# A two-layer diffusion trunk: conditioning transposes leave the fixed order of TensorE, their bias loads move up, the last norm is spread over three engines

## The chip, the core and the metric

The kernel runs on one core of a Trainium2 chip. The core has five engines with queues of their own: TensorE (PE, matrix products and transposes), VectorE (DVE), ScalarE (ACT), GpSimd (POOL) and SyncE (SP), whose queue issues most of the DMA transfers here. The metric is the device time of one execution in microseconds (us); less is better.

## The reference

The reference is a trunk of two layers over 512 latent tokens and 256 context tokens of width 1024. Each layer modulates a layer norm by a conditioning vector (adaLN), projects, runs four groups of heads side by side, projects back, adds a residual with a second norm, and then runs a modulated squared-ReLU MLP with a residual and a norm. Cut to what the change touches:

```python
def modulate(x, shift, scale):
    return layer_norm(x) * (1 + scale) + shift

mod = silu(c) @ w_ada + b_ada          # six vectors of 1024 per layer and stream
h = modulate(x, shift_1, scale_1)
y = concat(pool(h), windowed attention(h), latent attention(h), spatial gating(h)) @ w_out
x = layer_norm(alpha * x + gate_1 * y) * ln1_g + ln1_b
h = modulate(x, shift_2, scale_2)
x = layer_norm(alpha * x + gate_2 * (relu(h @ w_1) ** 2 @ w_2)) * ln2_g + ln2_b
```

The output is the latent stream behind layer two.

## The kernel before

All is float32. A product is made of three passes over parts `hi` and `lo` of both operands (`mm3`; every product has the line L133, every transpose L188, since helpers record them). Tokens are tiled by 128.

**Mixers.** The two attention groups run as units: one unit is one block of 128 queries of two heads, 24 units in layer 0 (latents and context) and 16 in layer 1 (latents alone). Loop pass x makes the scores of unit x (`s` and `sm`), transposes the probabilities of unit x-1 (`pT`), and makes the values of unit x-2 (`o`). `todo` holds projections of the latent attention (`uq`, `uk`) and the rotary work, each due at some x. `firsts[3]` is the unit at which the last pair of heads begins: 18 in layer 0, 12 in layer 1.

**Filler.** In each pass `fill(x, n)` also takes steps of `conditioning()`: a step loads 512 KB of the conditioning weights (`wada`, through SP's queue into one of four `raw` buffers) and makes 8 products `ada` of it. There are 40 steps in layer 0 and 24 in layer 1, paced so that they are spent two units ahead of the end. Sixteen steps make a block, for part of ada2 eight. At a block's end DVE adds the bias (`adaA = ada + badab`, L259; `badab` is loaded by four small DMAs, into a slot of the pool "T"), and `ada_cols` transposes the result into columns: up to four transposes `adaT` into one bank of PSUM, each copied out by DVE (`mc`, L275). Layer 0 has three blocks in its mixers, layer 1 two.

**What sets the order.** A scheduler orders each engine's instructions by its own estimates, except where the kernel chains them. While `self.pin` is set, every product and transpose is chained to the one before it in the order of the code (`pinned`), and the mixers set it for the whole loop. The pool `pa` has three PSUM banks of the tag "A", and `adaT`, `pT`, `uq`, `uk`, `o` and `wo` all draw on it. SP's queue runs in order: a load that waits for a free `raw` buffer holds up all that stand behind it, such as `rawwo` (weights of the output projection) and `rawz` (weights of the MLP).

**The last norm.** Behind the last MLP product each of four latent tiles takes: `fft = ff * gate` (DVE, L1266), `x += fft` (POOL for the last tiles, else DVE, L1267), statistics (L180, L182), the power -1/2 on POOL, then `affine_ln`: two operations on DVE per half (L328: subtract the mean, times g; L332: times the reciprocal deviation, plus b), and two DMAs of the output on SP's queue. `modT` transposes and modulates a normed tile, and ACT writes the result twice: rounded (`hi`, L377) and in full (`hfull`, L380).

The lines in which the block's bias and the pace stand:

```python
if u == 3 and i == len(part) - 1:
    bt = self.T("badab").rearrange("p (q x) -> p q x", q=4)
    for j in range(4):
        self.load(...)
wt = self.pr.tile([128, 2, 512], F32, name=self.nm("wada"), tag="raw")
...
want = (x + 1) * (24 if last else 40) // (n - 2) + 1
```

## Time and profile before

| | before |
|---|---|
| median of 3 runs | 1595.63 us (1595.61 to 1597.77) |
| profiled execution: time | 1597.13 us |
| profiled execution: span of the core | 1595.0 us |
| PE busy | 1496.2 us (94%) |
| DVE, ACT, POOL busy | 917.0, 567.1, 217.6 us |
| PE idle in the windows 160 to 320 us (mixers, layer 0) | 26.8 us |
| PE idle in the windows 1040 to 1200 us (mixers, layer 1) | 20.5 us |
| mean granted clock of PE | 0.974 |

The span runs from the first to the last instruction of the profile; the time of an execution has some 2 us more. Start times below count from the span's start. The granted clock is a share of the full 2.4 GHz: 1.00 is 2.4 and 0.50 is 1.2 GHz. An idle time in square brackets is the time for which the engine stood still just ahead of the instruction, with what released it.

### The profile page before, as it was taken

The numbers are of one execution on the slowest core, as the hardware profiler recorded it, in microseconds if no ns is written. First come the engines' busy times: TensorE is split into PE (matmuls) and PEld (weight loads), VectorE is DVE, ScalarE is ACT, GpSimd is POOL, SyncE is SP. The second block draws the span as 40 slices with busy tenths as digits, with TensorE's granted clock in tenths as the row PEclk, the third lists the DMA queues.
The fourth block names the chain that finished last, engine by engine and source line by source line (L and its number), as shares of the span: only waits on it lengthen the run. The fifth ranks groups of instructions, "written<-read, shape, count | busy, mean of one in ns | idle before, by whom it ended". The sixth has DMA issues, their size and how long they took to land. (4 is left out here: it accounts for less than half of the span.)

```text
span 1595.0 us, 23455 instructions
## 1 busy us (share of the span) xinstructions
PE 1496.2 (94%) x9438; PEld 1256.5 (79%) x9438; DVE 917.0 (57%) x1596; ACT 567.1 (36%) x1016; POOL 217.6 (14%) x243
## 2 busy tenths in 40 slices
PE   5999889799999999999999989979798999999996
PEld 3789667687898888888888868867676888888885
DVE  4484755547545455354554798666555555655557
ACT  4533444433731221212213157345434523223230
POOL 1011333213000000000000061143223000000003
PEclk9999899899999999999999999989899999999999
DMA  8531344652422122221212223224554333332321
GB/s 303 149 114 60 113 151 156 188 198 92 115 93 66 54 68 65 66 67 54 78 56 66 80 93 110 63 93 141 165 174 137 120 105 93 94 94 91 106 79 53
DMA packets 148068, 169.92 MB, mean 107 GB/s; under 512 B 8776, under 2 KB 96248, under 8 KB 147960
## 3 DMA queue, kind: packets, MB, share of 16 engines
q1 hardware_dynamic: 138488, 150.98, 30.5%
q10 hardware_dynamic: 9472, 17.45, 3.2%
q8 instruction: 74, 1.21, 0.3%
q14 instruction: 34, 0.28, 0.1%
HBM read 164.19 MB, written 4.22 MB: 106 GB/s over the span
## 5 line engine op out<-in xcount | busy, mean ns | idle before, releaser
L162 ACT ACTIVATE hiw<-raww 128x1024 fp32r<-128x1024 f32 x120 | 127.1, 1065 | 565.1 <-PE ff L133 565.1
L165 DVE TENSOR_TENSOR low<-raww,hiw 128x1024 fp32r<-128x1024 f32 x120 | 146.4, 1222 | 246.2 <-ACT hiw L162 246.2
L133 PE MATMUL ff<-low,fh 128*128 128x512 f32 x640 | 249.0, 389 | 0.0
L133 PE MATMUL ff<-hiw,fl 128*128 128x512 f32 x640 | 249.0, 389 | 0.0
L133 PE MATMUL ff<-hiw,fh 128*128 128x512 f32 x640 | 247.9, 389 | 0.0
L133 PE MATMUL ff<-hl,hiw 128*128 128x512 f32 (+1 forms) x672 | 237.9, 354 | 0.0
L133 PE MATMUL ff<-hh,hiw 128*128 128x512 f32 (+1 forms) x672 | 237.8, 354 | 0.0
L133 PE MATMUL ff<-hh,low 128*128 128x512 f32 (+1 forms) x672 | 237.7, 354 | 0.0
L1266 DVE TENSOR_TENSOR fft<-ff,gate 128x512 f32<-128x512 f32 x160 | 109.8, 686 | 100.3 <-PE ff L133 100.3
L133 PEld LDWEIGHTS ff<-hh,hiw 128*128 128x128 f32 x672 | 127.1, 189 | 18.0
L133 PEld LDWEIGHTS ff<-hl,hiw 128*128 128x128 f32 x672 | 127.1, 189 | 17.7
L133 PEld LDWEIGHTS ff<-hh,low 128*128 128x128 f32 x672 | 127.0, 189 | 17.5
L133 PEld LDWEIGHTS ff<-hiw,fl 128*128 128x128 f32 x640 | 120.2, 188 | 25.0
L133 PEld LDWEIGHTS ff<-hiw,fh 128*128 128x128 f32 x640 | 120.2, 188 | 24.8
L133 PEld LDWEIGHTS ff<-low,fh 128*128 128x128 f32 x640 | 120.2, 188 | 24.5
L1267 POOL TENSOR_TENSOR x<-x,fft 128x512 f32<-128x512 f32 x16 | 23.2, 1456 | 846.1 <-DVE fft L1266 841.1
L133 PE MATMUL ada<-wada,sc 128*32 128x128 f32 x1536 | 62.6, 302 | 26.1 <-DMA wada<-in_w_ada 26.1
L540 POOL TENSOR_SCALAR p<-p,rec 128x768 f32<-128x768 f32 (+3 forms) x80 | 60.9, 765 | 170.0 <-DVE rec L539 153.6
L1267 DVE TENSOR_TENSOR x<-x,fft 128x512 f32<-128x512 f32 x112 | 77.3, 690 | 2.9
L133 PEld LDWEIGHTS ada<-wada,sc 128*32 128x32 f32 x1536 | 42.5, 118 | 41.8 <-DMA wada<-in_w_ada 20.5
L133 PE MATMUL wo<-lowo,yh 128*128 128x512 f32 x160 | 62.5, 390 | 0.6 <-DVE lowo L165 0.6
L133 PE MATMUL wo<-hiwo,yh 128*128 128x512 f32 x160 | 62.4, 394 | 0.6 <-ACT hiwo L162 0.6
(331 smaller groups left out, 2761.4 us busy)
## 6 DMA issues: line engine op xcount, KB each, us to landing
raww<-in_w_ff SPq DMA_DIRECT2D x120, 512.0 KB, 4.2
wada<-in_w_ada SPq DMA_DIRECT2D x96, 512.0 KB, 4.2
rawwo<-in_w_out SPq DMA_DIRECT2D x16, 512.0 KB, 8.7
rawz<-in_w_ff SPq DMA_DIRECT2D x8, 512.0 KB, 6.7
rawwb<-in_w_in SPq DMA_DIRECT2D x12, 256.0 KB, 5.3
gate<-grow ACTq DMA_DIRECT2D x6, 512.0 KB, 4.7
badab<-in_b_ada SPq DMA_DIRECT2D x36, 64.0 KB, 4.6
x<-in_x SPq DMA_DIRECT2D x4, 512.0 KB, 4.2
```

The source lines that it names most:

```text
L133: return self.pinned(self.nc.tensor.matmul(out, lhsT, rhs, start=start, stop=stop))
L162: i = nc.scalar.activation(out=hi, in_=raw, func=AF.Copy)
L165: nc.vector.tensor_tensor(out=lo, in0=raw, in1=hi.bitcast(F32), op=ALU.subtract)
L540: nc.gpsimd.tensor_scalar(out=p[:, :keep], in0=p[:, :keep], scalar1=rec, scalar2=1.0, op0=ALU.mult, op1=ALU.mult)
L1266: nc.vector.tensor_tensor(out=t, in0=ps, in1=g[:, sl], op=ALU.mult)
L1267: eng.tensor_tensor(out=xt[:, sl], in0=xt[:, sl], in1=t, op=ALU.add)
```

## The change

1. `ada_cols` clears `self.pin` around its transposes and sets it again behind them: the chain runs past them, and the scheduler places them.
2. The four loads of a block's bias are issued at u = 0 of the block's last column piece, not at u = 3, so three steps earlier.
3. `load_heads` (weights of the latent attention's head projections) is called ahead of `sgu`, and splits a whole weight in two instructions on ACT and two on DVE, not in so many for each 128 of its rows.
4. The rotary work is due at x = 1 instead of 0, and what is due is now done behind `fill`.
5. `fill` is paced by `firsts[3]` (18 and 12) instead of n - 2 (22 and 14).
6. `modT` can share: for all calls but the first of the latents, every second full copy is made by DVE instead of ACT.
7. `affine_ln`: ACT scales and shifts, DVE multiplies by g, and b is added by POOL for the first half (by DVE for the second half, and for the last tile); the second half's output goes out through ACT's queue; the last tile's `x += fft` is on DVE.

```diff
                 for u in range(4):
-                    if u == 3 and i == len(part) - 1:
+                    if u == 0 and i == len(part) - 1:
                         bt = self.T("badab").rearrange("p (q x) -> p q x", q=4)
...
         nc = self.nc
+        pin, self.pin = self.pin, None
         if mc is None:
...
                 )
+        self.pin = pin
         return mc
...
-    def affine_ln(self, x, g, b):
+    def affine_ln(self, x, g, b, end):
         nc = self.nc
         m, rs = self.stats(lambda i: x[:, 512 * i:512 * i + 512], 2, EPS_R)
-        hs = [slice(512 * i, 512 * i + 512) for i in range(2)]
-        for h in hs:
-            nc.vector.scalar_tensor_tensor(
-                out=x[:, h], in0=x[:, h], scalar=m, in1=g[:, h], op0=ALU.subtract, op1=ALU.mult
-            )
-        for h in hs:
-            nc.vector.scalar_tensor_tensor(
-                out=x[:, h], in0=x[:, h], scalar=rs, in1=b[:, h], op0=ALU.mult, op1=ALU.add
-            )
+        nb = self.neg_mean(m, rs)
+        for i in range(2):
+            h = slice(512 * i, 512 * i + 512)
+            nc.scalar.activation(out=x[:, h], in_=x[:, h], func=AF.Identity, scale=rs, bias=nb)
+            nc.vector.tensor_tensor(out=x[:, h], in0=x[:, h], in1=g[:, h], op=ALU.mult)
+            eng = nc.vector if i or end else nc.gpsimd
+            eng.tensor_tensor(out=x[:, h], in0=x[:, h], in1=b[:, h], op=ALU.add)
...
-    def modT(self, xn, t0, t1, shift, scale, h, kts=range(KT), two=False):
+    def modT(self, xn, t0, t1, shift, scale, h, kts=range(KT), two=False, share=False):
...
             )
-            nc.scalar.activation(out=full[:, :n], in_=pt[:, :n], func=AF.Identity, scale=sc, bias=sh)
+            if share and kt % 2:
+                nc.vector.tensor_scalar(
+                    out=full[:, :n], in0=pt[:, :n], scalar1=sc, scalar2=sh, op0=ALU.mult, op1=ALU.add
+                )
+            else:
+                nc.scalar.activation(out=full[:, :n], in_=pt[:, :n], func=AF.Identity, scale=sc, bias=sh)
             nc.vector.tensor_tensor(out=lo, in0=full[:, :n], in1=hi.bitcast(F32), op=ALU.subtract)
...
+        def load_heads(src, cut, wide, name):
+            raw = self.pr.tile([128, src.shape[1], 4 * wide], F32, name=self.nm("raw" + name), tag="raw")
+            self.load(out=raw, in_=src)
+            hi, lo = (
+                self.pw.tile([128, src.shape[1], 4 * wide], F32R, name=self.nm(t + name), tag="W")
+                for t in ("hi", "lo")
+            )
+            r = raw.rearrange("p k (h c) -> p k h c", c=wide)
+            for a, b in ((0, cut), (cut, wide)):
+                h, w = (
+                    t[:, :, 4 * a:4 * b].rearrange("p k (h c) -> p k h c", c=b - a) for t in (hi, lo)
+                )
+                nc.scalar.activation(out=h, in_=r[:, :, :, a:b], func=AF.Copy)
+                nc.vector.tensor_tensor(
+                    out=w, in0=r[:, :, :, a:b], in1=h.bitcast(F32), op=ALU.subtract
+                )
+            return hi, lo
+        Wq = load_heads(A["mla_w_uq"][l].rearrange("(k p) n -> p k n", p=128), 64, 96, "uq")
+        Wk = load_heads(A["mla_w_ukv"][l].rearrange("(k p) n -> p k n", p=128), 64, 128, "ukv")
...
-        def load_heads(src, cut, wide, name):
-            raw = self.pr.tile([128, src.shape[1], 4 * wide], F32, name=self.nm("raw" + name), tag="raw")
-            self.load(out=raw, in_=src)
-            hi, lo = (
-                self.pw.tile([128, src.shape[1], 4 * wide], F32R, name=self.nm(t + name), tag="W")
-                for t in ("hi", "lo")
-            )
-            for k in range(src.shape[1]):
-                r = raw[:, k, :].rearrange("p (h c) -> p h c", c=wide)
-                for a, b in ((0, cut), (cut, wide)):
-                    h, w = (
-                        t[:, k, 4 * a:4 * b].rearrange("p (h c) -> p h c", c=b - a) for t in (hi, lo)
-                    )
-                    nc.scalar.activation(out=h, in_=r[:, :, a:b], func=AF.Copy)
-                    nc.vector.tensor_tensor(out=w, in0=r[:, :, a:b], in1=h.bitcast(F32), op=ALU.subtract)
-            return hi, lo
-        Wq = load_heads(A["mla_w_uq"][l].rearrange("(k p) n -> p k n", p=128), 64, 96, "uq")
-        Wk = load_heads(A["mla_w_ukv"][l].rearrange("(k p) n -> p k n", p=128), 64, 128, "ukv")
         VM = [self.X([128, 4, 256], "vmL"), self.X([128, 2, 256], "vmC")]
...
-        todo = {0: [rotary]}
+        todo = {1: [rotary]}
...
                 self.out_part(yL)
-            for st in todo.pop(x, []):
-                st()
             if x == n + 1:
...
                 values(x - 2)
-            fill(x, n)
+            fill(x, firsts[3])
+            for st in todo.pop(x, []):
+                st()
             if g is not None:
...
                     for n in range(2):
-                        ff2_tile(fs, Ws[n], n, tl, nc.gpsimd, self.last_mm if j + n else None)
+                        eng = nc.vector if l == DEPTH - 1 and j == len(tiles) - 1 else nc.gpsimd
+                        ff2_tile(fs, Ws[n], n, tl, eng, self.last_mm if j + n else None)
                     done(j)
...
             def fill(x, n):
-                want = (x + 1) * (24 if last else 40) // (n - 2) + 1
+                want = (x + 1) * (24 if last else 40) // n + 1
                 while spent[0] < want and next(steps, 0) is None:
...
                 self.modT(lambda i, kt: self.xn_cols(xn1[o + i], kt), t0, t1,
-                          col(mc[1], 8, s), col(mc[2], 0, s), hC if s else hL)
+                          col(mc[1], 8, s), col(mc[2], 0, s), hC if s else hL, share=s or t0 > 0)
...
                 if last:
-                    self.affine_ln(t, g2, b2)
-                    for h in (slice(0, 512), slice(512, 1024)):
-                        nc.sync.dma_start(out=self.out[128 * j:128 * j + 128, h], in_=t[:, h])
+                    self.affine_ln(t, g2, b2, j == LT - 1)
+                    for h, q in ((slice(0, 512), nc.sync), (slice(512, 1024), nc.scalar)):
+                        q.dma_start(out=self.out[128 * j:128 * j + 128, h], in_=t[:, h])
                     return
...
                 self.modT(lambda i, kt: self.xn_cols(xn[o + i], kt), t0, t1,
-                          col(mc0, 0, s), col(mc0, 8, s), hCn if s else hLn)
+                          col(mc0, 0, s), col(mc0, 8, s), hCn if s else hLn, share=s or t0 > 0)
```

**Where instructions move.** On PE, at the end of layer 0's third block, before. The names: `ada` are conditioning products, `adaT` the block's transposes, `sm` and `pT` the scores and the transposed probabilities of a unit, `o` its values.

```order
L133 MATMUL o_3427<-pT_3413,vmC_1751 64x128
L133 MATMUL o_3427<-pT_3412,vmC_1751 64x128
L133 MATMUL o_3427<-pT_3413,vmC_1751 64x128
L133 MATMUL ada_2893<-wada_3552,sc 32x128 x8
L188 MATMUL adaT_3564<-ident,adaA_2892 128x128 x4
L188 MATMUL pT_3573<-ident,p_3406 128x128 x4
L133 MATMUL sm_3579<-mkh_2768,qh_2764 128x256
L133 MATMUL sm_3579<-mkl_2769,qh_2764 128x256
L133 MATMUL sm_3579<-mkh_2768,ql_2765 128x256
L133 MATMUL sm_3591<-mkh_2770,qh_2766 128x256
```

The same place after:

```order
L133 MATMUL sm_3336<-mkh_2855,qh_2851 128x256
L133 MATMUL sm_3336<-mkl_2856,qh_2851 128x256
L133 MATMUL sm_3336<-mkh_2855,ql_2852 128x256
L188 MATMUL adaT_3312<-ident,adaA_2702 128x128
L188 MATMUL pT_3353<-ident,p_3247 128x128 x2
L188 MATMUL pT_3353<-ident,p_3259 128x128 x2
L133 MATMUL o_3360<-pT_3265,vmC_1747 64x128
L133 MATMUL o_3360<-pT_3266,vmC_1747 64x128
L133 MATMUL o_3360<-pT_3265,vmC_1747 64x128
L133 MATMUL o_3360<-pT_3266,vmC_1747 64x128
L188 MATMUL adaT_3312<-ident,adaA_2702 128x128
L133 MATMUL sm_3365<-mkh_2853,qh_2849 128x512
```

The four transposes stood in a row right behind the block's last products; now the first stands behind the scores of a unit, the second behind four value products, and the other two further on.

On PE in layer 1, at the end of its first block, before:

```order
L133 MATMUL o_10207<-pT_10341,v_9312 64x128
L133 MATMUL o_10207<-pT_10342,v_9312 64x128
L188 MATMUL adaT_10484<-ident,adaA_9726 128x128 x4
L133 MATMUL ada_10497<-wada_10498,sc 32x128 x8
L133 MATMUL ada_10497<-wada_10508,sc 32x128 x8
L188 MATMUL pT_10518<-ident,p_10335 128x128 x4
L133 MATMUL sm_10524<-mkh_10013,qh_10009 128x512
```

and after:

```order
L133 MATMUL o_10216<-pT_10203,v_9308 64x128
L133 MATMUL o_10216<-pT_10204,v_9308 64x128
L133 MATMUL ada_9697<-wada_10312,sc 32x128 x8
L188 MATMUL adaT_10324<-ident,adaA_9696 128x128
L133 MATMUL ada_10337<-wada_10338,sc 32x128 x8
L188 MATMUL pT_10348<-ident,p_10197 128x128 x4
L133 MATMUL sm_10354<-mkh_10055,qh_10051 128x512
```

Before, the four transposes stood in a row behind a unit's values; after, the first follows the block's last products directly, and the others stand among the scores of the next unit.

On SP's queue, around the bias of the same block of layer 0, before:

```order
L116 DMA wada_3450<-in_w_ada 128x2x512
L116 DMA rawwo_3466<-in_w_out 128x2x512
L116 DMA rawwo_3472<-in_w_out 128x2x512
L116 DMA rawwo_3478<-in_w_out 128x2x512
L116 DMA rawwo_3484<-in_w_out 128x2x512
L116 DMA wada_3552<-in_w_ada 128x2x512
L116 DMA rawz_3765<-in_w_ff 128x8x128
L116 DMA rawz_3776<-in_w_ff 128x8x128
L116 DMA badab_3547<-in_b_ada 32x4x128 x4
L116 DMA rawz_3787<-in_w_ff 128x8x128
L116 DMA rawz_3798<-in_w_ff 128x8x128
```

and after:

```order
L116 DMA wada_3215<-in_w_ada 128x2x512
L116 DMA wada_3225<-in_w_ada 128x2x512
L116 DMA wada_3290<-in_w_ada 128x2x512
L116 DMA wada_3300<-in_w_ada 128x2x512
L116 DMA badab_3210<-in_b_ada 32x4x128 x4
L116 DMA rawwo_3488<-in_w_out 128x2x512
L116 DMA rawwo_3494<-in_w_out 128x2x512
L116 DMA rawwo_3500<-in_w_out 128x2x512
L116 DMA rawwo_3506<-in_w_out 128x2x512
L116 DMA rawz_3761<-in_w_ff 128x8x128
```

The bias stood behind four loads of rawwo, the block's last load of wada and two of rawz; now it follows the block's last load of wada, and rawwo and rawz stand behind it.

## Rows read from the trace of the kernel before

**Rows 1.** Busy us by stretch and engine (instructions), then PE clock, DMA.

```profile
160.00:240.00 80.00, 67.35 (x737) 53.95 (x734) 50.31 (x129) 37.42 (x91) 24.56 (x34) 0.87 0.42 132
240.00:320.00 80.00, 65.85 (x771) 54.30 (x769) 42.51 (x89) 37.63 (x88) 24.44 (x32) 0.91 0.55 171
...
1040.00:1120.00 80.00, 68.75 (x745) 55.95 (x743) 52.98 (x119) 41.91 (x92) 32.91 (x41) 0.94 0.37 123
1120.00:1200.00 80.00, 70.78 (x565) 58.58 (x562) 39.68 (x67) 31.52 (x61) 16.30 (x16) 0.94 0.53 170
...
sum 1595.00, PE 1496.17 PEld 1256.48 DVE 916.98 ACT 567.08 POOL 217.62; mean PE 106.87 PEld 89.75 DVE 65.50 ACT 40.51 POOL 15.54
```

**Rows 2.** Waits of PE, 160 to 320 us: total us, times, longest.

```profile
PE adaT L188 <- DVE adaA L259: 8.6, 2, 6.0
PE ada L133 <- DMA wada<-in_w_ada: 3.6, 1, 3.6
...
PE adaT L188 <- DVE mc L275: 2.1, 7, 0.5
...
PE pT L188 <- ACT pT L548: 1.1, 1, 1.1
```

**Rows 3.** Waits of PE, 1130 to 1250 us.

```profile
PE adaT L188 <- DVE adaA L259: 7.1, 1, 7.1
...
PE hT L188 <- ACT hfull L380: 1.7, 2, 1.2
```

**Rows 4.** PE in time, 296 to 320 us: start, duration, instruction, [idle before].

```profile
296.60 0.65 PE L188 MATMUL pT<-ident,p 128*128 128x128 f32 x4
...
305.37 0.64 PE L133 MATMUL ada<-wada,sc 128*32 128x128 f32 x16 [3.58 <-DMA wada<-in_w_ada]
312.04 0.45 PE L188 MATMUL adaT<-ident,adaA 128*128 128x128 f32 x1 [6.03 <-DVE adaA L259]
...
314.49 1.06 PE L188 MATMUL pT<-ident,p 128*128 128x128 f32 x4
```

**Rows 5.** SP's queue in order of time, 288 to 312 us.

```profile
290.25 7.70 SPq L116 DMA_DIRECT2D rawwo<-in_w_out  x4
298.04 0.42 SPq L116 DMA_DIRECT2D wada<-in_w_ada  x1
298.55 4.89 SPq L116 DMA_DIRECT2D rawz<-in_w_ff  x2
303.49 3.17 SPq L116 DMA_DIRECT2D badab<-in_b_ada  x4
```

**Rows 6.** DVE in order of time, 309.5 to 314 us.

```profile
311.21 0.69 DVE L259 TENSOR_TENSOR adaA<-ada,badab 128x512 f32<-128x512 f32 x1 [4.48 <-DMA badab<-in_b_ada]
```

**Rows 7.** Busy time in shorter stretches, columns as in rows 1.

```profile
163.80:177.50 13.70, 11.61 (x42) 9.23 (x43) 10.10 (x21) 4.75 (x11) 1.99 (x2) 0.50 0.05 11
225.30:232.10 6.80, 6.41 (x38) 5.07 (x38) 2.26 (x8) 1.90 (x5) 0.30 (x1) 0.50 0.25 78
...
307.20:317.40 10.20, 4.58 (x18) 3.73 (x19) 2.85 (x8) 0.58 (x3) 0.53 (x1) 0.50 0.58 126
318.00:323.00 5.00, 5.00 (x65) 4.36 (x64) 2.11 (x7) 2.82 (x9) 1.62 (x4) 1.00 0.01 3
...
1143.50:1153.70 10.20, 6.54 (x24) 5.69 (x25) 3.64 (x7) 1.59 (x3) 0.00 (x0) 0.50 0.73 170
```

**Rows 8.** Waits of PE, 154 to 206 us.

```profile
PE s L133 <- ACT p L535: 2.8, 2, 2.1
```

**Rows 9.** Groups of instructions, 1290 to 1600 us: count, busy us, mean ns, idle.

```profile
L1267 POOL TENSOR_TENSOR x<-x,fft 128x512 f32<-128x512 f32 x8 | 11.0, 1377 | 342.4 <-DVE fft L1266 342.4
L332 DVE SCALAR_TENSOR_TENSOR x<-x,brs,ln2b 128x512 f32<-128x512 f32 x8 | 7.4, 955 | 0.0
```

**Rows 10.** DVE in order of time at the end, 1566 to 1595 us.

```profile
1589.24 1.40 DVE L328 SCALAR_TENSOR_TENSOR x<-x,bmv,ln2g 128x512 f32<-128x512 f32 x2
1590.56 1.41 DVE L332 SCALAR_TENSOR_TENSOR x<-x,brs,ln2b 128x512 f32<-128x512 f32 x2
```


## Prediction

> **What bounds the kernel now.** I read first the table of busy time by stretch, then who waits for whom in the two stretches that fall short, then the order of time around the longest waits, and last the clock. TensorE (PE) is busy for 1496.17 of 1595.00 us [rows 1], so the kernel can gain only where PE stands still or runs at a lower clock. Both happen in the mixers: from 160 to 320 us (layer 0) PE is idle for 12.65 + 14.15 us, from 1040 to 1200 us (layer 1) for 11.25 + 9.22 us, and the mean granted clock there is 0.87 to 0.94 [rows 1].
>
> The largest wait in both is one thing: the transposes adaT wait for the vector engine's (DVE) addition adaA, 8.6 us in layer 0 and 7.1 us in layer 1 [rows 2, 3]. The order of time shows why. The block's last conditioning product starts at 305.37 and takes 0.64 us; then PE waits 6.03 us for the first adaT [rows 4]. The addition that it waits for was itself waiting 4.48 us for the bias badab [rows 6]. The bias was issued only at 303.49, because SP's queue is first in, first out, and ahead of it stood four loads of rawwo (7.70 us) and two of rawz (4.89 us), each waiting for one of the four raw buffers [rows 5]. Behind the waiting transposes on PE stand pT and sm of the next unit, which need nothing of them; the pinned order holds them back.
>
> **The change, part by part.** The profiled run took 1597.13 us, its span 1595.0, so 2.1 us lie outside it; it is 1.5 us over the median of 1595.63, and I subtract from the median.
>
> *The bias, three steps earlier.* Four small issues move ahead of the block's last three loads in the code. In the new SP order they stand behind the block's last wada load, but ahead of rawwo and rawz. The whole queue in front of the bias in [rows 5], 290.25 to 298.04 and 298.55 to 303.44, is gone. The last wada load, which stood behind rawwo at 298.04 and for which PE waited 3.58 us at 305.37 [rows 4, 5], is ahead of rawwo as well. What waits behind the bias now is rawwo, later by the four issues' time, 3.17 us with the wait for a free slot of the bias in it [rows 5]; its user, the output projection, begins behind the mixers' last unit, so that is free.
>
> *The transposes, unpinned.* In the new PE order the four stand singly, behind the scores, probabilities or products of the next unit. What they cover: in layer 0's last block 16 ada and 12 sm matmuls lie between the last load's arrival and the first adaT, about 3 us, and the addition with its wait takes 0.69 us once the bias is there [rows 6]. I go by this: the stall ends. The DVE copies mc (2.1 us of short waits, seven of them [rows 2]) now have other matmuls between them too. In two of the five blocks (layer 0's second, layer 1's first) the first adaT still stands right behind the last ada group; there PE waits for one addition, 0.69 us and the way there, about 1 us each, from [rows 6].
> Removed: 8.6 + 7.1 (adaT for adaA), 3.6 (ada for wada, layer 0), 2.1 (mc) = 21.4; left over 2 x 1.0: **-19.4 us**.
>
> *The clock.* PE's clock is granted at half (the 1.2 of its 1.2 and 2.4 GHz) for 6.8, 10.2 and 10.2 us right around or behind the three longest adaT waits, in the stretches from 225.3, 307.2 and 1143.5 [rows 7]. PE was busy there for 6.41 + 4.58 + 6.54 = 17.53 us. Four pT take 0.65 us at the full clock and 1.06 at half [rows 4], so 39% of that busy time is lost, 6.8 us; at exactly half speed it would be 8.8. I take **-7.5**, since without the idle before it the fall has no cause in view. Against it: the stretch from 225.3 followed a wait of 2.55 us only, so shorter idle may do.
>
> *Earlier filler and later rotary.* Conditioning is spread over 18 and 12 units, not over all 24 and 16; loads of head weights (load_heads) precede sgu, with fewer and larger splits; the rotary work comes one unit later. At the start of the mixers PE waits for ACT's softmax (s, 2.8 us [rows 8]) and runs at half clock from 163.8 to 177.5, idle for 2.09 us and losing about 39% of 11.61 = 4.5 us [rows 7]. New filler stands there. But DVE is busy for 10.10 of those 13.70 us [rows 7] and its work stays, so most waits do: **-3** over both layers, between 0 and -10. The units without filler cost nothing: from 318 to 323, with no ada in it, PE is busy for 5.00 of 5.00 us at full clock [rows 7].
>
> *A bank held longer.* adaT holds one of three "A" banks of PSUM for about a unit, now that its four transposes are spread; o holds another through a whole head pair, and pT, uq and uk then share the third. The trace of before has no wait for that; nearest is pT behind ACT's copy of the pT before, 1.1 us, once [rows 2]. Zero if the copies are quick enough, five blocks x 1.1 = 5.5 if each meets one such wait: about the middle, **+2.5**, since the copies run on two engines in turn.
>
> *The last norm.* Before, DVE did eight L328 and eight L332, the latter 955 ns in the mean [rows 9]. After, ACT scales, DVE multiplies by g, and b is added on POOL for the first half of three tiles, else on DVE. The last tile's chain gains one small DVE operation and two changes of engine, and DVE still does both halves' product and sum: 4 x 0.69 (an addition of that size [rows 6]) against 1.40 + 1.41 [rows 10], no gain. POOL takes 1377 ns for such an addition [rows 9], and x of the last tile leaves POOL for DVE. By hand along the new DVE order the last tile ends about 1 us later: **+1** (-2.5 to +2.5).
> What the rows show against this part: L332 takes 955 ns in the mean, but two take 1.41 us when POOL rests [rows 9, 10], so it is DVE beside a working POOL that is slow. The Trainium skill ("SBUF — State Buffer", section "Who interferes with whom") says that a DVE instruction with two SBUF inputs contends with a GpSimd instruction that reads SBUF, and that one blocks the other fully; the trace agrees, and by the rule three more POOL additions would add some 2 us to the tail instead of 1.
>
> *The rest.* Half of the second copies of modT go to DVE (hT waits of 1.7 us [rows 3] shrink by perhaps 0.5 twice); the last four loads of ada2 still stand behind the output projection's, so their wait stays; start-up is as before: **-1** (-2.5 to +1).
>
> Sum: -19.4 - 7.5 - 3 + 2.5 + 1 - 1 = **-27.4**, so 1595.6 - 27.4 = **1568.2 us**.
>
> **The rivals.**
> A, *the stalls go, the clock stays*: PE's shorter leftover waits still bring half clock, as 2.55 us did, and the early stage gives nothing. Then -19.4 + 2.5 + 1 - 1 = -16.9, 1579.
> B, *the early stage opens too*: filler covers the waits for softmax and the clock stays up. Layer 0 has 2.09 + 4.5 + 2.8 = 9.4 us there [rows 7, 8]; layer 1 from 1040 to 1120 has 11.25 idle and a clock of 0.94, some 4 us more [rows 1]. Half of that 24.7 instead of 3 gives 9.3 more: 1559. For it: x=1's scores and ada stand among the early work; against it, DVE's load there.
> C, *it moves and does not help*: PE still takes its matmuls in order, so a transpose waits wherever it stands. If the bias or its addition (behind other DVE work, 1.2 us pieces) comes later than I think, each block's wait is only moved. The waits of 21.4 and the clock would then shrink by a fifth at most: 1590 to 1595. Against it: in [rows 4 to 6] all but 0.69 us of the wait is the bias's place in the queue, and that place changes. The Trainium skill ("TensorE: Matmul & The Clock Gate", section "Step-by-step: what each phase is for") says that only weight loads are pulled ahead and matmuls stay in program order; the trace agrees (nothing of pT passes the 6.03 us), and by this rule alone the transposes' new place, without the earlier bias, would give little.
> D, *slower*: the faster fill outruns the raw buffers. A load issued at 298.04 was there at 305.37, 7.3 us later [rows 4, 5]; up to three steps in a unit, with four buffers, can leave PE waiting in each filled unit, and each wait can bring half clock. There are 30 filled units; from 31 us / 30 = 1.05 us each the gain is gone and it is slower, at 1.2 us each 1604. Against it: 40 steps in 18 units of some 6.4 us (5.00 [rows 7] and 2.2 x 0.64 [rows 4]) need one load in 2.9 us, and four buffers at 7.3 us each give one in 1.8.
>
> **How the numbers follow.** Forecast (1562 to 1573) 0.50, B 0.17, A 0.20, C 0.06, D 0.07. The likeliest gives 1568.2. Unknown bounds (early stage to -10, bank to +5.5, tail, rest) reach from 1555 to 1576; A with its bank at +5.5 reaches 1582. Range 1555 to 1582, which leaves out C, D and a part of B. A measurement here can tell about 0.2% (3.2 us): faster 0.88, same 0.05 (most of C), slower 0.07.
>
> **What would show it.** In the profile after: no adaT wait over 1 us and no bias issue behind rawwo; full clock at 225, 307 and 1143 in the same place of the program; idle in the layer 0 mixers near 12 instead of 27 us; the tail behind PE's last matmul 10 to 11 us long, as before. Wrong if waits of adaT for adaA over 2 us remain, if ada waits for wada in the filled units (D), or if half clock falls on other places in the mixers (A).

## The result, and the profile after

The changed kernel takes 1571.51 us (median of 4 runs, 1570.16 to 1572.89) against 1596.70 for the kernel before (4 runs): a ratio of 0.9842, interval 0.9825 to 0.9859. That is 25.2 us less; forecast were 27.4 less, 1568.2 in a range of 1555 to 1582. The profiled run after took 1570.16 us with a span of 1568.4.

Where the time went is read by stages, each from the first PE instruction of its kind to that of the next (read off the order of time; the last one ends with the span):

| stage (us) | before | after | change | forecast |
|---|---|---|---|---|
| start to the first `s` | 154.6 | 159.9 | +5.3 | "as before" |
| mixers, layer 0 (`s` to `wo`) | 168.6 | 151.7 | -16.9 | -27.4 with layer 1 |
| mixers, layer 1 | 124.0 | 111.4 | -12.6 | (in the row above) |
| `wo` to `ff`, layers 0 and 1 | 132.4 | 130.8 | -1.6 | -1 with the next two and the start |
| MLP of layer 0 (`ff` to the next `hT`) | 546.7 | 543.1 | -3.6 | (in the row above) |
| projections, layer 1 (`hT` to `s`) | 98.5 | 99.0 | +0.5 | (in the row above) |
| MLP of layer 1 and the last norm | 370.2 | 372.5 | +2.3 | +1 |
| span | 1595.0 | 1568.4 | -26.6 | |

The mixers' forecast is the sum of four terms: -19.4 for the stalls, -7.5 for the clock, -3 for the early stage, +2.5 for the bank. They gave 29.5 us, a little more, and the two ends of the program, forecast at about 0 and +1, took 7.6 back. In the mixers both of the things that the prediction tells apart changed: idle time and the clock. Three kernels' busy time over just their two mixers, before, after, and the experiment e3 of below, which has only the unpinned transposes and the early bias (columns as in [rows 1]; busy PE first, the clock third from the end):

```profile
154.60:323.20 168.60, 140.92 (x1599) 114.84 (x1597) 98.16 (x233) 80.73 (x194) 51.49 (x68) 0.90 0.46 144
1038.50:1162.50 124.00, 104.49 (x1125) 86.54 (x1124) 76.73 (x163) 63.37 (x136) 43.51 (x52) 0.92 0.40 125
```

```profile
160.00:311.50 151.50, 133.21 (x1597) 109.51 (x1597) 94.70 (x233) 81.99 (x193) 52.67 (x68) 0.97 0.51 161
1024.00:1135.00 111.00, 98.58 (x1122) 81.05 (x1121) 76.69 (x163) 63.13 (x135) 44.29 (x52) 1.00 0.44 139
```

```profile
160.10:317.30 157.20, 136.50 (x1598) 112.15 (x1597) 97.72 (x233) 81.31 (x194) 51.47 (x68) 0.92 0.50 155
1031.00:1145.30 114.30, 101.51 (x1122) 84.16 (x1121) 76.03 (x163) 62.98 (x134) 43.50 (x52) 0.96 0.44 135
```

PE has the same work in all three, so a smaller busy time is a higher clock. Before, PE was idle for 27.7 + 19.5 = 47.2 us and busy for 245.4. After, it is idle for 18.3 + 12.4 = 30.7 and busy for 232.3 (the rows after leave out 0.5 us at the edges of the stages): 16.5 us less idle time and 13.1 less through the clock. PE was at half clock for 54.6 us of the two mixers before, and for 10.2 us after.

The waits of PE in the two mixers after, layer 0 first (us in total, times, longest); they answer to [rows 2] and to the first of [rows 3]:

```profile
PE pT L188 <- ACT pT L555: 2.9, 4, 1.3
PE adaT L188 <- DVE adaA L259: 2.7, 2, 2.0
PE s L133 <- ACT p L542: 1.7, 2, 1.0
PE adaT L188 <- DVE mc L276: 1.6, 2, 1.4
```

```profile
PE adaT L188 <- DVE adaA L259: 2.6, 2, 1.8
PE s L133 <- ACT p L542: 2.0, 2, 1.4
PE pT L188 <- ACT pT L555: 1.4, 2, 0.7
...
PE adaT L188 <- DVE mc L276: 0.8, 1, 0.8
```

The waits of 6.0 and 7.1 us for adaA are gone, and so is ada's wait for wada. What is left of adaT's waits is 2.7 + 1.6 + 2.6 + 0.8 = 7.7 us, more than the 2.0 of the forecast. Around the third block of layer 0, SP's queue, then DVE, then PE, in order of time:

```profile
269.60 1.84 SPq L116 DMA_DIRECT2D badab<-in_b_ada  x4
275.00 5.09 SPq L116 DMA_DIRECT2D rawwo<-in_w_out  x4
282.64 7.10 SPq L116 DMA_DIRECT2D rawz<-in_w_ff  x4
```

```profile
281.39 1.23 DVE L165 TENSOR_TENSOR lowo<-rawwo,hiwo 128x1024 fp32r<-128x1024 f32 x1 [3.20 <-ACT hiwo L162]
282.53 0.68 DVE L146 TENSOR_TENSOR yl<-o,yh 128x512 fp32r<-128x512 f32 x1
283.13 0.68 DVE L259 TENSOR_TENSOR adaA<-ada,badab 128x512 f32<-128x512 f32 x1
283.73 1.22 DVE L165 TENSOR_TENSOR lowo<-rawwo,hiwo 128x1024 fp32r<-128x1024 f32 x1
284.86 1.82 DVE L533 TENSOR_REDUCE nmax<-sm 128x1 f32<-128x768 f32 x2
286.59 0.16 DVE L276 TENSOR_SCALAR mc<-adaT 128x8 f32<-128x8 f32 x1
```

```profile
278.51 1.08 PE L133 MATMUL ada<-wada,sc 128*32 128x128 f32 x32
...
283.87 0.33 PE L188 MATMUL adaT<-ident,adaA 128*128 128x128 f32 x1 [1.98 <-DVE adaA L259]
...
286.80 0.47 PE L188 MATMUL adaT<-ident,adaA 128*128 128x128 f32 x1 [1.41 <-DVE mc L276]
```

The bias is issued at 269.60, ahead of rawwo and rawz, where [rows 5] had it behind them. At 283.13 the addition does not wait for it: it carries no bracket. The block's last products end at 279.59, and the addition starts 3.5 us later because it waits its turn on DVE. The instruction ahead in DVE's order is a split `lowo`, and for that one DVE stands idle until 281.39 (its bracket: 3.20 us for ACT's `hiwo`); then come `lowo` itself, 1.23 us, and `yl`. The copy mc at 286.59 stands behind another split and two `nmax`. The output projection's loads now come early enough for their splits to stand among the block's last steps on DVE. PE's clock is at half from 284.9 to 291.7 us after that: one stretch is left of the three that [rows 7] has behind adaT.

### The profile page after: what moved, and what is told of

Its sections match the earlier page's. It is cut to its first block, busy times and chain, and to the rows that moved or that the text cites. A ratio compares the mean times of both kernels' runs of the same rounds, so it can differ in the third digit from the quotient of the medians.

```text
span 1568.4 us, 23456 instructions
## 1 busy us (share of the span) xinstructions
PE 1481.3 (94%) x9438; PEld 1246.7 (79%) x9438; DVE 922.7 (59%) x1615; ACT 565.7 (36%) x1000; POOL 222.0 (14%) x244
## 3 DMA queue, kind: packets, MB, share of 16 engines
q1 hardware_dynamic: 137912, 149.94, 30.7%
## 4 chain that ended last, share of the span: by engine, by line
PE 84%; DVE 7%; DMA 3%; ACT 2%; issue 1%; POOL 1%; SPq 0%; ACTq 0%; POOLq 0%; DVEq 0%
PE ff L133 54%; PE wo L133 5%; PE wb L133 3%; PE o L133 3%; PE pT L188 2%; PE wa L133 2%; PE ada L133 2%; PE wp L133 2%; PE wu L133 2%; PE wq L133 2%; PE sm L133 2%; DMA wada<-in_w_ada 1%; DVE nmax L533 1%; PE wk L133 1%; PE hT L188 1%
## 5 line engine op out<-in xcount | busy, mean ns | idle before, releaser
L133 PEld LDWEIGHTS ada<-wada,sc 128*32 128x32 f32 x1536 | 41.8, 116 | 34.1 <-DMA wada<-in_w_ada 13.1
L188 PE MATMUL pT<-ident,p 128*128 128x128 f32 x368 | 55.9, 279 | 9.9 <-ACT pT L555 4.4
```

The costliest lines, as they stand in the source:

```text
L133: return self.pinned(self.nc.tensor.matmul(out, lhsT, rhs, start=start, stop=stop))
L188: return self.pinned(self.nc.tensor.transpose(out, in_, self.ident if ident is None else ident))
```

## Experiments

All were timed beside runs of the kernel before on the same chip; a ratio below 1 is faster than the kernel before.

**Which of the two halves ends the stalls.** e1 is the kernel before with the transposes unpinned:

```diff
+        pin, self.pin = self.pin, None
...
+        self.pin = pin
```

> The kernel before with the transposes adaT unpinned and nothing else; the bias loads stay at their late place. Theory (the bias's place in SP's queue makes the stalls, PE takes its order as it stands): the first adaT of each block still stands right behind the block's last products, and waits 5 to 7 us for the addition in layer 0's third and layer 1's second block; only the short waits between transposes go, about 2 us: 1592 to 1596 us. Rival (the pinned order makes the stalls): the waits of adaT for adaA fall below 2 us, the half clock behind them goes, 1575 to 1582 us.

Measured: 1590.62 us, ratio 0.9959 (0.9946 to 0.9973). Waits of PE in layer 0's mixers:

```profile
PE adaT L188 <- DVE adaA L259: 7.9, 2, 5.6
PE ada L133 <- DMA wada<-in_w_ada: 2.7, 1, 2.7
```

and in layer 1's:

```profile
PE adaT L188 <- DVE adaA L259: 7.2, 1, 7.2
```

The addition still holds adaT for 7.9 us in layer 0 (8.6 in [rows 2]) and for 7.2 at layer 1's second block (7.1 in [rows 3]). The time came out 1 to 2 us below what the theory had and 9 above the rival: the pinned order did not make the long waits. Pinned or not, PE stands at the first transpose for as long as the bias is late.

e2 is the kernel before with the early bias only:

```diff
-                    if u == 3 and i == len(part) - 1:
+                    if u == 0 and i == len(part) - 1:
```

> The kernel before with the bias loads three steps earlier and nothing else; the transposes stay in a pinned row. Theory (place in the queue): the bias has landed when the last products end, so a block waits about 1 us for the addition and 0.3 to 0.7 us between transposes; ada's 3.6 us for wada in layer 0 goes too; the mixers lose 15 to 20 us of time. At the start the earlier bias costs 4 to 5 us, as in the changed kernel: 1581 to 1586 us in all. Rival (the pinned order makes the stalls): waits of adaT for adaA stay over 4 us, 1592 to 1600 us.

Measured: 1587.98 us, ratio 0.9954 (0.9938 to 0.9970).

```profile
PE adaT L188 <- DVE mc L275: 2.3, 7, 0.5
PE ada L133 <- DMA wada<-in_w_ada: 1.9, 1, 1.9
PE adaT L188 <- DVE rec L539: 1.8, 1, 1.8
...
PE adaT L188 <- DVE adaA L259: 1.1, 1, 1.1
```

These are waits of layer 0's mixers; the wait for adaA itself is down to 1.1 us, once there (8.6 in [rows 2]), and in layer 1 no wait is put down to it, so the place of the bias in the queue was the cause of the long waits. But the gain is 2 to 7 us short of what the theory had: the transposes in a row still stop PE for each copy mc (2.3 us) and for DVE work ahead of the addition (1.8, put down to `rec`), and half clock still follows at all three places of [rows 7] (3.4 us from 230, 6.8 each from 309 and 1142). In the mixers PE is idle for 35.4 us, 11.8 less than before, but busy for 247.0, no less than before.

e3 has both edits and nothing else of the change.

> The kernel before with both: transposes unpinned, bias three steps earlier; old pace of the filler, old order of head weights and rotary work, old last norm, no sharing in modT. Theory: adaT's waits shrink to about 1 us a block, half clock at those places goes: the mixers lose 20 to 24 us, the start costs 5: 1576 to 1581 us. If the filler's pace and the early stage carry much of the gain instead, as a rival has it, it stays over 1584.

Measured: 1578.25 us, ratio 0.9888 (0.9870 to 0.9907), as the theory had it. Together the two give 17.0 us; alone they gave 4.6 and 7.2. Each removes one of two reasons for PE to stop at the same place. In the rows above, e3 is idle for 20.7 + 12.8 = 33.5 us in the mixers, 13.7 less than before, and busy for 238.0, 7.4 less. Little of the clock comes back with one of them alone: in the two mixers PE is at half clock for 54.6 us before, 44.4 in e1, 51.2 in e2 and 34.1 in e3. The stretches from 225 and 1143 of [rows 7] are gone in e3. The third is still 10.2 us long, from 302.3, and stands now at another wait of layer 0's third block:

```profile
PE ada L133 <- DMA wada<-in_w_ada: 4.5, 1, 4.5
```

That wait was 3.6 us before [rows 2], so neither the early bias nor the unpinned order removes it.

**What gave the rest of the mixers' gain.** e5 is the changed kernel with the old pace:

```diff
-            fill(x, firsts[3])
+            fill(x, n)
...
-                want = (x + 1) * (24 if last else 40) // n + 1
+                want = (x + 1) * (24 if last else 40) // (n - 2) + 1
```

> The changed kernel with the old pace of the filler (40 steps over 22 units, 24 over 14); early order of head weights and rotary, unpinned transposes, early bias, new norm stay. Theory (the pace keeps the last conditioning loads ahead of the output projection's in the raw buffers): with the old pace PE waits again 2 to 5 us for the last wada of layer 0's third block, and half clock follows there; from sm to wo layer 0 takes 74 to 76 us and not 69, layer 1 about 1 more: 1576 to 1580 us. Rival (the early order of head weights and rotary work made that gain): within 1570 to 1574.

Measured: 1574.8 us, ratio 0.9874 (0.9855 to 0.9894), between the two. The wait for wada is back (2.5 us at 294.90), yet the two mixers take 150.6 + 112.2 us in its profile where the changed kernel takes 151.7 + 111.4: what was lost at their end was saved in the units before, which carry fewer products. That profile is of e5's fastest execution, 1570.08 us. Its median is 2 to 3 us above the two that the changed kernel has (1571.51 here, 1572.60 in e12 below), and its interval overlaps the changed kernel's. So what the pace is worth is not settled: nothing to some 3 us. What the run does show is that the pace ends ada's wait for wada: the wait is back with the old pace and nothing else.

e8 is the changed kernel with `load_heads` behind `sgu` in its old form (left out of the cut below) and the rotary work at x = 0 ahead of `fill`:

```diff
-        todo = {1: [rotary]}
+        todo = {0: [rotary]}
...
+            for st in todo.pop(x, []):
+                st()
...
             fill(x, firsts[3])
-            for st in todo.pop(x, []):
-                st()
```

> The changed kernel with head weights loaded behind sgu again, in the old small instructions, and the rotary work at x = 0 ahead of the filler; pace and all else as changed. Theory (this part opened the early stage: less half clock behind the first waits of both mixers, though little waiting less): 2 to 5 us come back between the first s and the first sm of the two layers, 1573 to 1577 us. Rival (the early stage's clock was kept up by the denser filler alone): 1570 to 1573.

Measured: 1580.41 us, ratio 0.9903 (0.9887 to 0.9918), 8 to 9 us above the changed kernel and more than the theory had. From the first `s` to the first `sm` it takes 84.5 and 63.3 us in the two layers; the changed kernel takes 82.6 and 58.5. The 2 us of layer 0 are no more than one program varies by there (last section); layer 1's 58.4 to 58.5 stand in all eight profiles that have this part and the new pace, so its 4.8 us are a difference. 18 us near the start of layer 1's mixers, e8 and then after (busy PE, instructions; the clock third from the end; e8's row begins 1.8 us behind its first `s`, and counted from that `s` it has 12.94 us busy at 0.80, which reads the same):

```profile
1031.70:1049.70 18.00, 13.13 (x85) 10.03 (x85) 12.35 (x28) 8.34 (x18) 3.97 (x4) 0.75 0.00 1
```

```profile
1023.80:1041.80 18.00, 15.30 (x177) 11.67 (x175) 15.84 (x38) 10.37 (x25) 6.09 (x7) 1.00 0.25 90
```

In e8 PE is idle for 4.87 us, after for 2.70, and after it has done twice as many instructions by then (177 against 85) at a clock of 1.00 where e8 has 0.75: in e8 PE still waits 2.6 us in one piece for `krT`, as before the change; after, conditioning products and the next unit's scores stand there. Over both mixers as a whole e8 is idle for 16.1 + 14.3 = 30.4 us, no more than after's 30.7, and busy for 240.2 against 232.3, with 34.1 us at half clock against 10.2. What this part gave is clock: it moves work between waits, and hardly removes one.

**The start.** After, the first `s` comes 5.3 us later. Around 56 to 66 us, before and after:

```profile
56.00:66.00 10.00, 8.87 (x47) 7.01 (x46) 3.44 (x7) 6.98 (x11) 0.00 (x0) 1.00 0.37 106
```

```profile
56.00:66.00 10.00, 5.56 (x17) 4.30 (x16) 4.53 (x5) 6.23 (x8) 0.00 (x0) 0.68 0.86 261
```

PE after, ACT after, and SP's queue, before and then after:

```profile
51.80 1.95 PE L133 MATMUL ada<-wada,sc 128*32 128x128 f32 x64
...
60.63 0.80 PE L133 MATMUL wb<-hiwb,hh 128*128 128x512 f32 x1 [4.44 <-ACT hh L379]
```

```profile
57.38 1.06 ACT L162 ACTIVATE hiwb<-rawwb 128x1024 fp32r<-128x1024 f32 x1 [10.60 <-DMA rawwb<-in_w_in]
...
59.82 0.76 ACT L379 ACTIVATE hh<-hT,mc 128x512 fp32r<-128x512 f32 x1
```

```profile
41.88 1.95 SPq L116 DMA_DIRECT2D rawwb<-in_w_in  x4
```

```profile
52.50 3.17 SPq L116 DMA_DIRECT2D rawwb<-in_w_in  x4
```

PE waits for `hh`, which stands on ACT behind the splits `hiwb`, and those waited for the load rawwb. It was issued at 41.88 before and at 52.50 after. In the changed order PE makes the last 32 products `ada` of the program's first block (64 records in the trace, two for each) in one piece behind the products wb, at 51.80, so the raw buffers that their weights fill come free that much later. This is the earlier bias again, in a block that is made ahead of the mixers, where there is no pinned order.

e4 puts the bias of that block alone back:

```diff
-                    if u == 0 and i == len(part) - 1:
+                    if u == (3 if (l, g) == (0, 0) else 0) and i == len(part) - 1:
```

> The changed kernel with the bias of the very first block, loaded at the start of the program ahead of the mixers, back at u = 3; all else as changed. Theory (at the start the earlier bias makes the scheduler put four groups of ada products behind the wb products, which holds the raw buffers and so delays rawwb): the first s starts at 155 instead of 160 us, PE's wait of wb for hh falls from 4.4 to about 1 us, and the whole takes 1565 to 1568 us. Rival (the loss at the start is of another part, such as DMA timing): no change, 1570 to 1573.

Measured: 1569.8 us, ratio 0.9829 (0.9804 to 0.9853). The wait for hh is 0.87 us and the clock stays up at 60 us, as expected, but the first `s` came at 158.6, and the time is not clear of the changed kernel's. The start also varies from one profile to the next (the eighth group of products `ada` begins at 22.44 us before and at 23.97 in e4), so it takes several: with the early bias at the start, eight of them (after, e2, e3, e5 to e8, e12) have the first `s` at 158.9 to 161.9, in the mean 160.4; with the late one, six (before, e1, e4, e9 to e11) have it at 153.7 to 158.6, in the mean 155.5. The difference of 4.9 us is what the earlier bias costs there.

**The last norm.** e6 is the changed kernel with the old `affine_ln`, both halves of the output on SP's queue and the last tile's `x` on POOL:

```diff
-            nc.scalar.activation(out=x[:, h], in_=x[:, h], func=AF.Identity, scale=rs, bias=nb)
-            nc.vector.tensor_tensor(out=x[:, h], in0=x[:, h], in1=g[:, h], op=ALU.mult)
-            eng = nc.vector if i or end else nc.gpsimd
-            eng.tensor_tensor(out=x[:, h], in0=x[:, h], in1=b[:, h], op=ALU.add)
+            nc.vector.scalar_tensor_tensor(
+                out=x[:, h], in0=x[:, h], scalar=m, in1=g[:, h], op0=ALU.subtract, op1=ALU.mult
+            )
...
```

> The changed kernel with the old last norm as a whole: two operations on DVE per half, the last tile's x on POOL, both halves of the output through SP's queue. Theory (the new norm made the tail longer: POOL's addition of b for the third tile holds the last tile's power on POOL for 1 us, and the chain gains a DVE operation and a step on ACT): the time from PE's last matmul to the end of the span is 12.6 us as before the change, not 14.8; the whole 1568 to 1570.5 us. Rival (that tail length is chance of the one profile): it stays at 14 to 15 us and the whole at 1570 to 1573.

Measured: 1570.31 us, ratio 0.9855 (0.9835 to 0.9876). The time alone can't tell this from the changed kernel, but the tail can. PE's last matmul starts at 1553.24 after and at 1554.83 in e6:

```profile
1553.24 0.39 PE L133 MATMUL ff<-hiw,fl 128*128 128x512 f32 x1
```

```profile
1554.83 0.39 PE L133 MATMUL ff<-hiw,fl 128*128 128x512 f32 x1
```

The spans are 1568.4 and 1567.9, so from the end of that matmul 14.7 and 12.6 us follow; before the change it was 12.6. The six profiles with the new norm all have 14.7, the eight with the old one all 12.6. The end after, on POOL, ACT and DVE:

```profile
1558.92 1.71 POOL L335 TENSOR_TENSOR x<-x,ln2b 128x512 f32<-128x512 f32 x1 [2.86 <-DVE x L333]
1560.59 0.99 POOL L173 TENSOR_TENSOR brs<-rv,mhalf 128x1 f32<-128x1 f32 x1
```

```profile
1561.81 1.52 ACT L332 ACTIVATE x<-x,nmr,brs 128x512 f32<-128x512 f32 x2 [3.35 <-DVE nmr L313]
```

```profile
1559.43 0.15 DVE L172 TENSOR_SCALAR rv<-bmv 128x1 f32<-128x1 f32 x1
...
1561.62 0.16 DVE L313 SCALAR_TENSOR_TENSOR nmr<-bmv,brs 128x1 f32<-128x1 f32 x1 [0.44 <-POOL brs L173]
1562.66 1.40 DVE L333 TENSOR_TENSOR x<-x,ln2g 128x512 f32<-128x512 f32 x2 [0.88 <-ACT x L332]
1563.97 1.29 DVE L335 TENSOR_TENSOR x<-x,ln2b 128x512 f32<-128x512 f32 x2
```

The power of the last tile needs only `rv`, done at 1559.58; it starts at 1560.59, because POOL is adding b to the third tile until then. So the last chain loses 1.0 us there. The larger loss is the order of the norm itself. Before, the last tile's `rv` stood here, with its L328 right behind it and its L332 at 1590.56 [rows 10]:

```profile
1589.17 0.15 DVE L172 TENSOR_SCALAR rv<-bmv 128x1 f32<-128x1 f32 x1
```

L328 needs only the mean and ran while POOL made the power, so only L332, 1.41 us, stood behind the power. After, the step on ACT needs the power, and both products and both sums on DVE stand behind it. From the end of `rv` to the end of the last `x` it took 2.7 us before and takes 5.7 after. Up to `rv`, the tail gained 1.0 us (6.9 before, 6.0 after, from the end of PE's last matmul), where `x` of the last tile is on DVE now.

**Both together, and one more.** e9 is the changed kernel with e4's and e6's edits.

> The changed kernel with the very first block's bias late again (as in e4) and the old last norm (as in e6). Theory: both gains add, 3 to 5 us at the start and 2 at the end, less what the start varies by: 1565 to 1568 us, below the changed kernel. Rival (either is chance): 1569 to 1572.

Measured: 1565.59 us, ratio 0.9811 (0.9793 to 0.9829), and once more beside the changed kernel on one chip, as e11 and e12:

> The kernel of e9 once more, beside e10 and the changed kernel on one chip: 1564 to 1567 us.

> The changed kernel itself once more, beside e9's and e10's kernels on one chip. Theory (start and tail each cost it something): 4 to 7 us above e11. Rival: within 2 us of it.

Measured: e11 1565.38 us, ratio 0.9812 (0.9794 to 0.9831); e12 1572.60, ratio 0.9855 (0.9835 to 0.9874). The difference is 7.2 us, and the intervals are apart: the two losses of the change are real together, and the kernel without them has the lowest median of all that ran.

e10 goes after the waits of adaT that are left. It is e9 with the splits of the output projection's first weights ordered behind the PE instruction at which the code asks for them:

```diff
-            self.load_w([((slice(None),), w[:, k:k + 2, 0:512])], [128, 2, 512], "wo") for k in self.OUT_ORDER
+            self.load_w([((slice(None),), w[:, k:k + 2, 0:512])], [128, 2, 512], "wo", gate=self.pin) for k in self.OUT_ORDER
```

> The kernel of e9 with one more change: the splits hiwo and lowo of the output projection's first four weight pieces are ordered behind the PE instruction at which the code asks for them, so that on DVE they stand behind the third block's addition adaA and its copies mc and no longer between them. Theory (the waits of adaT that remain in the changed kernel, 2.0 and 1.4 us in layer 0 and 1.8 in layer 1, come from four splits of 1.2 us on DVE ahead of adaA and mc): these waits fall below 0.8 us each, the half clock of 6.7 us behind them goes, 3 to 6 us less than e9: 1560 to 1563 us where e9 takes 1565.6. Rival (they come from the bias or the products): waits and time as in e9.

Measured: 1570.42 us, ratio 0.9835 (0.9817 to 0.9853): 5 us slower than e11 beside it, though their intervals overlap in part. The mechanism was right and the forecast wrong. The waits for adaA did fall, from 5.4 us in all in e11 to 2.7, and no half clock follows the third block of layer 0. But the splits now stand between the row maxima and the reciprocals of layer 1's last units; pT waits for POOL, POOL for DVE's reciprocal, and the clock falls behind that:

```profile
1129.51 0.66 PE L188 MATMUL pT<-ident,p 128*128 128x128 f32 x4 [1.86 <-POOL p L548]
```

```profile
1131.00:1143.00 12.00, 11.62 (x59) 9.17 (x60) 0.42 (x1) 0.98 (x2) 0.90 (x1) 0.72 0.24 70
```

The second row is a stretch of 12 us right behind those waits: PE is busy for 11.62 of them at a clock of 0.72. The wait moved to another consumer of the same engine. In e10's profile, layer 1's mixers and the output projection behind them take 2.0 + 2.3 us more than in e11's; what else made up the 5 us is not shown.

e7 is the changed kernel with modT's copies all on ACT:

```diff
-            if share and kt % 2:
+            if False and kt % 2:
```

> The changed kernel with modT's full copies all on ACT again. Theory (the sharing shortens hT's waits for hfull by some 0.6 us at two places, at most one stretch of half clock): 0.5 to 3 us slower than the changed kernel beside it. Rival (it moves nothing): within 0.5 us of it.

Measured: 1577.38 us, ratio 0.9883 (0.9866 to 0.9901): 4.8 us above e12 beside it (the intervals overlap a little), more than either expected. Its profile shows one of hT's waits for hfull in layer 0 back at 1.3 us (0.7 in e12) and the MLP of layer 0 at 543.8 us, 1.5 longer than e12's and 0.7 longer than after's; the rest of the difference lies in the mixers, where layer 0 takes 156.9 and 151.7 us and layer 1 114.2 and 111.3, as more half clock at waits that are nearly the same. Whether the sharing brings that about, or one profile shows it by chance, stays open.

## Why the prediction held, point by point

- **The stalls (-19.4).** Right in mechanism for the 15.7 us of adaT for adaA: e2 shows that the place of the bias made them, and e1 that unpinning alone leaves them. The size was too large: with e3's two edits the mixers' idle time falls by 13.7 us, with the whole change by 16.5. Two steps were off. One is "left over 2 x 1.0": 7.7 us of adaT's waits are left, since the addition and the copies stand behind splits on DVE. Rival C named that mechanism ("behind other DVE work, 1.2 us pieces") but for its cover I looked at PE's order only. The other is ada's wait for wada, 3.6, which I credited to the early bias: it is 4.5 in e3, and goes only with the new pace (e5).
- **The clock (-7.5).** e3's busy time in the mixers is 7.4 us less. The mechanism is right, the close number in part luck: two of the three stretches are gone in e3, a shorter one from 256 us as well, while the third is as long as before, behind the wait for wada. In the whole change it is 6.8 us long, behind a wait of 1.98, so rival A's doubt holds in part.
- **Early filler and later rotary (-3, to -10).** Undersized. e8 puts this part at 8 to 9 us, and in the mixers all of it is clock: of rival B the clock came true and the covered waits did not. The pace itself is worth nothing to some 3.
- **A bank held longer (+2.5).** pT's waits for ACT's copy grew from 1.1 us to 2.9 + 1.4 = 4.3 in the mixers, 3.2 more, near the term. But four of the six, 3.5 of the 4.3 us, begin (at 229.21, 250.95, 271.50 and 1077.15 us) when no adaT is being written or copied, and before the change pT at 250.41 and uk at 269.25 already waited 1.13 and 0.71 us for the same copies. So the number came near by luck, and no run here shows that adaT's bank costs anything like it.
- **The last norm (+1).** It cost 2.1 us by the tails of after and e6. The step that was off is the count of what stands behind the power: I set four operations of DVE against two, 2.76 against 2.81 us, and did not see that L328 had run beside the power. The nearer price was the one by the Trainium skill's rule ("SBUF — State Buffer", section "Who interferes with whom"), some 2 us. The trace agrees with the rule in one place, and the price came near by luck: a DVE addition beside POOL's takes 1.63 us (at 1559.55; one at 1554.98, with no addition on POOL, 0.67), but it belongs to the third tile and ends before the last tile's power does. What the last tile waits for is POOL's own queue and the longer chain.
- **The rest (-1).** Wrong in "start-up is as before": the start lost 4.9 us. The order of PE showed the products in one piece there, and I costed the earlier bias in the mixers' blocks only, not in each block that the same line serves. The sharing of modT, which I put at 1, is worth 4.8 by the times, but only 0.7 to 1.5 show in the MLP of layer 0. That MLP gave 3.6 us in all, and no run here accounts for the rest.
- **The signs.** By its own list the prediction held in part. The bias is ahead of rawwo, the clock is full at the places of 225 and 1143, and in the mixers no ada waits for wada. But three waits of adaT are over 1 us (1.98, 1.41, 1.80), the longest just under the 2 us that I had called wrong and 2.14 in e12's profile of the same program, and layer 0's mixers are idle for 18.3 us, not near 12. The tail was 12.6 us before, not the 10 to 11 that I wrote. And in rival D the gain of 27.4 us is used up from 0.91 us a unit, not 1.05.
- **The sum.** -27.4 forecast, -25.2 measured: errors of 3 to 5 us in both directions cancelled, so that it came this close is luck.

## What to carry to other kernels

When PE waits for a small load, look first at what stands ahead of that load in its queue: here four small DMAs behind weight loads that nobody needed yet cost two waits of 6 and 7 us, and moving them with the instruction that needs them was worth more than either alone. Follow such an edit through every place that the same line serves, since a load that helps in one block can hold buffers in another. A queue that runs in order can hold a short step even while its engine is idle: here a ready addition stood behind a split that waited for its load. And when a wait is removed by moving work on a shared engine, name who stands behind that work in its new place before counting the gain.

## What the hardware showed that was not expected

The clock decides a large part of such a change. Up to PE's last matmul the stretches at half clock add up to some 75 us before and 41 after, and 13.1 of the 29.5 us that the mixers gave came through it, not through idle time. It also differs between executions of one kernel: from 168 to 182 us the profiles of e9 and e11, the same program, show

```profile
168.00:182.00 14.00, 11.57 (x93) 9.91 (x94) 9.61 (x22) 5.29 (x12) 4.60 (x4) 0.88 0.34 109
```

```profile
168.00:182.00 14.00, 12.10 (x79) 10.03 (x80) 7.33 (x18) 4.58 (x10) 3.58 (x4) 0.63 0.28 85
```

a mean clock of 0.88 and 0.63, and the stage from the first `s` to the first `pl` takes 41.3 and 43.6 us. A difference of 2 us in one stage of one profile is therefore no evidence of its own.
